# A hybrid DeltaNet and sliding-window decoder layer: the framework sorts each engine's instructions by its finer clock instead of its simple one

## The chip, the cores and the metric

The kernel runs on one core of a Trainium2 chip. The core has engines that each work through their own list of instructions in order: PE (matrix products), ACT (scalar functions), DVE (vector operations), POOL (a second, slower vector engine) and SP, which issues all DMA transfers of this kernel. An instruction that waits holds up everything behind it on its engine. The metric is the time of one execution in microseconds (us) on the device; the time of a kernel is the median of its runs.

## The reference, cut to what matters

The layer takes x (2048 rows of 1024) and computes, in fp32:

```
xn  = rms_norm(x)                                # 2048 x 1024
p   = xn @ w_in                                  # q,k,v of the DeltaNet, z gates, q,k,v of attention, branch gates
A   = gated delta rule over chunks of 64 (conv, l2 norm, triangular solve, scan over the chunks), 4 heads
B   = dilated sliding-window attention, 4 heads x 3 groups (dilation 1, 4, 16), merged by their softmax denominators
y   = sigmoid(g0) * ((norm(A) * silu(zA)) @ w_branch_dn) + sigmoid(g1) * ((B * silu(zB)) @ w_branch_swa)
out = x + y @ w_out
```

## The kernel before, in words

The program text is a list of stages. Every large product is done in three passes on two-part operands (a high part `hh`, `wh`, `oh`, `mh` and a rest `hl`, `wl`, `ol`, `ml`), which stand as three lines each in the profile.

1. **Attention** (`swa`): 12 units (3 groups x 4 heads) of 16 steps. A step projects 128 rows to q, k and v with 24 products of 128x384 (`s_proj`, L176 to L178, into a tile `mm`), normalises them (`s_norm`), and takes earlier rows through the attention in small pieces between the products: transposes of q and k (`a_trans`, L231, tile `tp`), scores (`a_score`, L249 to L251, or L246 in the last group, tile `sc`), row maximum on DVE (L253, L256), the exponential on ACT (L258, tile `p`), transposes of `p` (`a_ptrans`, L265), a copy of them on ACT (L267, tile `pT`), the product with v (`a_pv`, L273 and L274, tile `po`), a copy and a store (L276, L279). The weights of the next unit come meanwhile as 256 KB pieces (tile `raw`, three buffers) and are split into two parts by ACT (L79) and by DVE or POOL (L80).
2. **Column units** (`cunits`): 36 units of 128 columns of `w_in`, four blocks of 512 rows each, 24 products of 128x512 a block (L413 to L415). Small work is hung between these products by a table of events: the last attention items, the DeltaNet's gates (`ab_math`), for each of four heads the convolution (L510 to L521), the transposes of k (L552, tile `tp`, taken on by ACT in L556 and L557) and the k and q products (L598 to L601), the triangular inverse on DVE, the scan (16 steps: L729 and L731, L740, L746, L751 on PE, L733, L748 and L754 on DVE, L736, L742 and L758 on ACT, a store in L769).
3. **Prologue of the end**: when the scan has stored its last rows, its memory is given to the end stage. `o_load` loads a tile of DeltaNet output (`od`, L861) and one of attention output (`oc`, L838, one buffer), `combine` merges the three groups on DVE (L843 to L855, tile `osw`), `o_prep` transposes both (L870), multiplies them by the gates z (L871) and splits them (L874 on ACT, L875 on POOL) into `oh` and `ol`. Beside it the weights of the end are loaded in 32 pieces (L824, `raw` and `raw2`, three buffers each) and split (L831 on ACT, L833 on DVE or POOL) into the memory of `hh` and `hl`, which the column units read until their last blocks.
4. **End**: eight blocks of 256 rows; `fin_y` has 24 products of 128x256 for each of eight column blocks (L886 to L888, then L890 on DVE, L893, L894), `fin_out` the output product (L903 to L905) and the store (L910).

Dependencies become semaphores, and tiles with a few buffers make a later instruction wait for the last reader of the buffer. The framework does not keep the order of the text: it simulates the engines with a clock and hands out, of the instructions that are ready on its clock, the one of the highest priority; the order in which they come out is the fixed order of each engine's list. PSUM tiles are few: `mm` has 3 buffers, `tp` 2, `sc` 2, `po` 1.

```python
            a["kqT"] = self.sp.tile([P, 2, P], F32, name="kqT", bufs=1)
...
        oc = fp.tile([P, G, H, 130], F32, name="oc", bufs=1)
...
        raw = self.fp.tile([P, 4, P], F32, name="raw2", bufs=3) if k0 else self.rawp.tile([P, 4, P], F32, name="raw")
```

## Time and profile before

| | |
|---|---|
| time, median of 3 runs | 2415.41 us (2414.24 to 2415.93) |
| the profiled execution | 2419.78 us, 4.37 us above the median |
| its span, first to last instruction | 2417.9 us |
| granted clock of PE, mean | 0.993 |
| instructions on PE | 13710 products and as many weight loads |
| busy | PE 98%, DVE 48%, ACT 35%, POOL 34% of the span |

In the profiled execution the attention runs from the start to about 1003 us, the column units from there to about 2030 us (their products are mixed with the last attention items until about 1140 us, the four heads until about 1460 us, the inverse until about 1740 us, the scan until about 1916 us, the prologue of the end until about 1952 us) and the end stage from 2030 us on. Rows of the profile are read thus: a start time, a duration, the engine, the line and the operation, what is written and what is read, and in square brackets the idle time of the engine just before with what ended it. Since products overlap on PE, the time from one start to the next is what a product costs, not its duration.

### The profile page before, as it was taken

What the parts mean: (1) busy time and instruction counts of PE and PEld (TensorE: products, weight loads), DVE (VectorE), ACT (ScalarE), POOL (GpSimd) and SP (SyncE); (2) the same over time, 40 slices, a digit from 0 to 9 for tenths busy, and PEclk for the clock granted to TensorE, in tenths of its full rate; (3) what the DMA queues carried; (4) which work ended last, traced back from release to release, by engine and by line L of the source; (5) the groups of instructions that cost most, each with busy time, mean ns of one, the idle gap of its engine ahead of it and who ended that gap; (6) DMA issues with size and microseconds to landing.
All of it is one profiled execution on the core that took longest, in us unless ns stands there. A gap on an engine that the chain in (4) does not pass through costs nothing.

```text
span 2417.9 us, 40142 instructions
## 1 busy us (share of the span) xinstructions
PE 2365.4 (98%) x13710; PEld 2151.0 (89%) x13710; DVE 1163.6 (48%) x2738; ACT 848.3 (35%) x2985; POOL 824.2 (34%) x1785
## 2 busy tenths in 40 slices
PE   7999999999999999999999999999999999999999
PEld 7999999999999999987777878888888878889998
DVE  5644433233343433343766665999444433454431
ACT  5644433243443333322665662111243313111110
POOL 4433334433333343420433541111133212442441
PEclk9999999999999999999999999999999999999999
DMA  5211102233333333433444443222566655555542
GB/s 158 76 44 39 31 23 66 92 98 95 113 104 96 109 114 96 108 104 97 128 121 123 112 115 111 79 75 72 179 199 195 184 162 155 160 182 156 151 139 75
DMA packets 348819, 274.22 MB, mean 113 GB/s; under 512 B 57864, under 2 KB 317256, under 8 KB 348232
## 3 DMA queue, kind: packets, MB, share of 16 engines
q1 hardware_dynamic: 348616, 271.66, 38.7%
q8 instruction: 109, 1.79, 0.3%
q14 instruction: 94, 0.77, 0.1%
HBM read 167.47 MB, written 104.10 MB: 112 GB/s over the span
## 4 chain that ended last, share of the span: by engine, by line
PE 83%; DMA 6%; DVE 4%; ACT 3%; POOL 2%; issue 2%; SPq 1%; DVEq 0%; ACTq 0%; POOLq 0%
PE mm L176 10%; PE mm L178 10%; PE mm L177 10%; PE mm L413 9%; PE mm L415 8%; PE mm L414 8%; PE mm L903 2%; PE mm L905 2%; PE mm L904 2%; PE mm L886 2%; PE mm L888 2%; DMA gcb<-gcscr 2%; PE mm L887 2%; PE po L274 2%; PE tp L231 2%
## 5 line engine op out<-in xcount | busy, mean ns | idle before, releaser
L176 PE MATMUL mm<-wh,hh 128*128 128x384 f32 (+1 forms) x1536 | 555.5, 362 | 2.7 <-ACT hh L119 2.0
L178 PE MATMUL mm<-wh,hl 128*128 128x384 f32 (+1 forms) x1536 | 521.0, 339 | 0.0
L177 PE MATMUL mm<-wl,hh 128*128 128x384 f32 (+1 forms) x1536 | 520.6, 339 | 0.2 <-POOL wl L80 0.2
L413 PE MATMUL mm<-hh,wh 128*128 128x512 f32 x1152 | 468.0, 406 | 0.0
L415 PE MATMUL mm<-hh,wl 128*128 128x512 f32 x1152 | 457.1, 397 | 0.0
L414 PE MATMUL mm<-hl,wh 128*128 128x512 f32 x1152 | 454.6, 395 | 0.0
L176 PEld LDWEIGHTS mm<-wh,hh 128*128 128x128 f32 x1536 | 291.4, 190 | 5.7 <-ACT hh L119 2.4
L177 PEld LDWEIGHTS mm<-wl,hh 128*128 128x128 f32 x1536 | 292.2, 190 | 0.6 <-POOL wl L80 0.6
L178 PEld LDWEIGHTS mm<-wh,hl 128*128 128x128 f32 x1536 | 290.7, 189 | 0.0
L415 PEld LDWEIGHTS mm<-hh,wl 128*128 128x128 f32 x1152 | 218.6, 190 | 47.1
L413 PEld LDWEIGHTS mm<-hh,wh 128*128 128x128 f32 x1152 | 219.0, 190 | 44.3
L414 PEld LDWEIGHTS mm<-hl,wh 128*128 128x128 f32 x1152 | 218.9, 190 | 42.0
L80 POOL TENSOR_TENSOR wl<-raw,wh 128x512 fp32r<-128x512 f32 (+1 forms) x75 | 107.5, 1445 | 406.0 <-ACT wh L79 405.8
L199 DVE SCALAR_TENSOR_TENSOR rec<-mm,st,wqk 128x128 f32<-128x128 f32 x256 | 78.0, 347 | 265.0 <-POOL st L197 256.0
L195 POOL TENSOR_SCALAR st<-st 128x2 f32<-128x2 f32 x192 | 45.2, 235 | 424.3 <-ACT rec L191 288.8
L258 ACT ACTIVATE p<-sc,ol 128x128 f32<-128x128 f32 (+1 forms) x192 | 81.9, 427 | 297.8 <-DVE ol L256 284.1
L886 PE MATMUL mm<-oh,hh 128*128 128x256 f32 x512 | 143.9, 281 | 3.0 <-DVE gt L890 3.0
L888 PE MATMUL mm<-oh,hl 128*128 128x256 f32 x512 | 143.0, 279 | 0.0
L887 PE MATMUL mm<-ol,hh 128*128 128x256 f32 x512 | 143.0, 279 | 0.0
L518 DVE SCALAR_TENSOR_TENSOR acc<-xr,cw,acc 128x512 f32<-128x512 f32 x144 | 121.7, 845 | 42.3 <-ACT acc L516 38.2
L197 POOL TENSOR_TENSOR st<-st,mhalf 128x2 f32<-128x2 f32 x192 | 134.7, 701 | 16.0
L79 ACT ACTIVATE wh<-raw 128x512 fp32r<-128x512 f32 (+1 forms) x145 | 90.0, 631 | 110.2 <-PE mm L414 73.8
(240 smaller groups left out, 4317.9 us busy)
## 6 DMA issues: line engine op xcount, KB each, us to landing
raw<-in_w_in_dram SPq DMA_DIRECT2D x144, 256.0 KB, 3.4
rscr<-rec SPq DMA_DIRECT2D x128, 192.0 KB, 1.9
qk<-rscr SPq DMA_DIRECT2D x128, 128.0 KB, 2.2
gscr<-gt SPq DMA_DIRECT2D x64, 256.0 KB, 2.4
gt<-gscr SPq DMA_DIRECT2D x64, 256.0 KB, 3.5
oscr<-ol SPq DMA_DIRECT2D x192, 65.0 KB, 1.9
oc<-oscr SPq DMA_DIRECT2D x16, 780.0 KB, 5.6
rec<-rec SPq DMA_DIRECT2D x16, 768.0 KB, 5.4
```

The lines of the kernel that those rows point to most:

```text
L80: eng.tensor_tensor(out=l, in0=raw, in1=h.bitcast(F32), op=ALU.subtract)
L176: nc.tensor.matmul(pr[:, :w], a, wh[:, k, :w], start=(k == 0), stop=False)
L177: nc.tensor.matmul(pr[:, :w], a, wl[:, k, :w], start=False, stop=False)
L178: nc.tensor.matmul(pr[:, :w], b, wh[:, k, :w], start=False, stop=(k == KT - 1))
L197: nc.gpsimd.tensor_tensor(out=st[:, 2:4], in0=st[:, 0:2], in1=self.mhalf[:, 0:2], op=ALU.pow)
L413: nc.tensor.matmul(pr, wh[:, k, :], a, start=(k == 0), stop=False)
L414: nc.tensor.matmul(pr, wh[:, k, :], b, start=False, stop=False)
L415: nc.tensor.matmul(pr, wl[:, k, :], a, start=False, stop=(k == KT - 1))
L518: nc.vector.scalar_tensor_tensor(out=acc, in0=xr[:, j:j + 512], scalar=w[:, j:j + 1], in1=acc, op0=ALU.mult, op1=ALU.add)
L886: nc.tensor.matmul(o, self.wbh[:, k, ms], oh[:, k, :], start=(k == b * 4), stop=False)
L887: nc.tensor.matmul(o, self.wbh[:, k, ms], ol[:, k, :], start=False, stop=False)
L888: nc.tensor.matmul(o, self.wbl[:, k, ms], oh[:, k, :], start=False, stop=(k == b * 4 + 3))
```

## The change

One argument is added, which makes the framework's sorting use another clock: one that models instructions and transfers with finer durations, the transfers' among them.

```diff
     out = nc.dram_tensor("out_0_dram", (1, T, D), F32, kind="ExternalOutput").ap()
-    with tile.TileContext(nc) as tc:
+    with tile.TileContext(nc, schedule_with_timeline_sim=True) as tc:
         with ExitStack() as ctx:
             Net(ctx, tc, ins, out).run()
```

The instructions stay the same: 12897 products and transposes on PE, 1354 transfers, and the same operations on DVE, ACT and POOL. What changes is their order on each engine, and with it which of them carry a wait. Three places of the new order follow. A name with a number is one buffer's use (`po_6588`), `x2` stands for two like instructions in a row.

**Place 1, attention, in the seventh unit, on PE.** `mm_6551` and `mm_6620` are the projections of two successive steps; L273 and L274 multiply `pT_6561` (made by ACT in L267) with v. Before:

```order
L176 MATMUL mm_6551<-wh_5841,hh_67 128x384
L177 MATMUL mm_6551<-wl_5842,hh_67 128x384
L178 MATMUL mm_6551<-wh_5841,hl_68 128x384
L273 MATMUL po_6588<-v_6220,pT_6561 128x128
L274 MATMUL po_6588<-v_6290,pT_6561 128x128
L231 MATMUL tp_6593<-ident_69,qk_6427 128x128 x2
```

The same product in the new order:

```order
L178 MATMUL mm_6620<-wh_5841,hl_68 128x384
L176 MATMUL mm_6620<-wh_5841,hh_67 128x384
L177 MATMUL mm_6620<-wl_5842,hh_67 128x384
L273 MATMUL po_6588<-v_6220,pT_6561 128x128
L274 MATMUL po_6588<-v_6290,pT_6561 128x128
L265 MATMUL tp_6627<-ident_69,p_6580 128x128 x2
```

It has moved from one step's projection into the next step's, behind 20 more products of 128x384 in all; between the transposes `tp_6558` (L265), from which `pT_6561` is copied, and L273 stand 21 projection products and two transposes now, where there were 12 and three score products.

On ACT, the copy L267 and the splits L79 of the next unit's weights at that place, before:

```order
L79 ACTIVATE wh_6963<-raw_7180 128x4x128
L191 ACTIVATE rec_6536,st_6535<-mm_6484 128x128 x2
L192 ACTIVATE rec_6536<-mm_6484 128x128
L79 ACTIVATE wh_6963<-raw_7253 128x4x128
L267 ACTIVATE pT_6561<-tp_6558 128x256
L79 ACTIVATE wh_6963<-raw_7326 128x4x128
```

and now:

```order
L79 ACTIVATE wh_6963<-raw_7180 128x4x128
L258 ACTIVATE p_6512,ol_6509<-sc_6505,ol_6509 128x256
L191 ACTIVATE rec_6536,st_6535<-mm_6484 128x128 x2
L192 ACTIVATE rec_6536<-mm_6484 128x128
L79 ACTIVATE wh_6963<-raw_7253 128x4x128
L79 ACTIVATE wh_6963<-raw_7326 128x4x128
L267 ACTIVATE pT_6561<-tp_6558 128x256
```

One more split and one exponential stand ahead of the copy.

**Place 2, the last attention items, on PE, among the column units.** Before, with blocks of column products between the pieces:

```order
L274 MATMUL po_13788<-v_13575,pT_13763 128x128
L231 MATMUL tp_13792<-ident_69,qk_13665 128x128 x2
L413 MATMUL mm_13754<-hh_67,wh1_13493 128x512
L414 MATMUL mm_13754<-hl_68,wh1_13493 128x512
L415 MATMUL mm_13754<-hh_67,wl1_13494 128x512
L413 MATMUL mm_13754<-hh_67,wh1_13493 128x512
L414 MATMUL mm_13754<-hl_68,wh1_13493 128x512
L415 MATMUL mm_13754<-hh_67,wl1_13494 128x512
L265 MATMUL tp_13805<-ident_69,p_13780 128x128
```

Now:

```order
L415 MATMUL mm_14116<-hh_67,wl1_13749 128x512
L274 MATMUL po_13735<-v_13526,pT_13710 128x128
L246 MATMUL sc_13775<-kqT_13742 128x128
L265 MATMUL tp_13761<-ident_69,p_13727 128x128
L231 MATMUL tp_13792<-ident_69,qk_13665 128x128 x2
L274 MATMUL po_13788<-v_13575,pT_13763 128x128
L246 MATMUL sc_13824<-kqT_13795 128x128
L265 MATMUL tp_13805<-ident_69,p_13780 128x128
L231 MATMUL tp_13841<-ident_69,qk_13712 128x128 x2
L274 MATMUL po_13837<-v_13617,pT_13807 128x128
```

The items have moved behind later column blocks (`mm_14116`, where they stood in `mm_13754`), and the last nine follow one another with no column product between them.

**Place 3, the end of the scan, on PE and DVE.** L746 is the scan's last product, L870 the transposes for the end, L886 the end's first product. Before, on PE, the last product of the scan:

```order
L746 MATMUL po_20970<-vn_20957,rec_20800 128x128 x2
L751 MATMUL tp_20954<-vn_20957,rec_20800 128x128 x2
L751 MATMUL tp_20959<-vn_20962,rec_20800 128x128 x2
L746 MATMUL po_20990<-vn_20962,rec_20800 128x128 x2
L413 MATMUL mm_20947<-hh_67,wh1_20030 128x512
```

then 492 column products, with the first four tiles' L870 behind 78, 84, 96 and 108 of them, and at last:

```order
L414 MATMUL mm_21708<-hl_68,wh1_21504 128x512
L415 MATMUL mm_21708<-hh_67,wl1_21505 128x512
L886 MATMUL mm_21784<-oh_21151,hh_67 128x256
L887 MATMUL mm_21784<-ol2_21152,hh_67 128x256
L888 MATMUL mm_21784<-oh_21151,hl_68 128x256
```

Now, in one piece:

```order
L415 MATMUL mm_21708<-hh_67,wl1_21505 128x512
L740 MATMUL tp_20959<-rr_20933,vb1_18949 128x128 x2
L746 MATMUL po_20970<-vn_20957,rec_20800 128x128 x2
L751 MATMUL tp_20954<-vn_20957,rec_20800 128x128 x2
L751 MATMUL tp_20959<-vn_20962,rec_20800 128x128 x2
L746 MATMUL po_20990<-vn_20962,rec_20800 128x128 x2
L870 MATMUL tp_21155<-ident_69,od_21023 128x128 x4
L870 MATMUL tp_21173<-ident_69,osw_21035 128x128 x4
L870 MATMUL tp_21199<-ident_69,od_21103 128x128 x4
L886 MATMUL mm_21784<-oh_21151,hh_67 128x256
```

`mm_21708` is the last column block. The scan starts where it started and ends right behind the last column product; the first product of the end follows it directly. 36 products of the end come next, and only then the L870 of `osw_21115`, the second attention tile. On DVE the updates of the state (L748) and of the output (L754) in the last step, before:

```order
L733 SCALAR_TENSOR_TENSOR rr_20933<-sc_20931,ksn_13082,rec_20800 128x128 x2
L748 SCALAR_TENSOR_TENSOR S0_18940<-S0_18940,eglb_13080,po_20970 128x128
L748 SCALAR_TENSOR_TENSOR S1_18941<-S1_18941,eglb_13080,po_20970 128x128
L754 TENSOR_TENSOR qs_20921<-tp_20954,qs_20921 128x256
L754 TENSOR_TENSOR qs_20932<-tp_20959,qs_20932 128x256
```

and now:

```order
L733 SCALAR_TENSOR_TENSOR rr_20933<-sc_20931,ksn_13082,rec_20800 128x128 x2
L833 TENSOR_TENSOR hl_68<-raw_21893,hh_67 128x4x128
L833 TENSOR_TENSOR hl_68<-raw_21901,hh_67 128x4x128
L833 TENSOR_TENSOR hl_68<-raw_21940,hh_67 128x4x128
L833 TENSOR_TENSOR hl_68<-raw_21979,hh_67 128x4x128
L748 SCALAR_TENSOR_TENSOR S0_18940<-S0_18940,eglb_13080,po_20970 128x128
L748 SCALAR_TENSOR_TENSOR S1_18941<-S1_18941,eglb_13080,po_20970 128x128
L754 TENSOR_TENSOR qs_20921<-tp_20954,qs_20921 128x256
L833 TENSOR_TENSOR hl_68<-raw_22036,hh_67 128x4x128
L754 TENSOR_TENSOR qs_20932<-tp_20959,qs_20932 128x256
```

Splits of the output weights (L833, pieces `raw_...` in three buffers, each split by ACT in L831 first) stand ahead of the scan's last updates; before they stood behind the end's first L890. The splits of the `raw2` pieces stand likewise among the rows of `combine`. In the four heads, in the stretch between places 2 and 3, the second to fourth pairs of L552 of heads two to four stand 1.1 to 4 us of products later on PE than before, and L600 1.8 to 2.5 us later; the column units under the inverse keep their order.

## The prediction

> **What bounds the kernel.** I read the page's first lines and its chain, then the waits of PE, then tables by stage.
>
> ```profile
> span 2417.9 us, 40142 instructions
> PE 2365.4 (98%) x13710; PEld 2151.0 (89%) x13710; DVE 1163.6 (48%) x2738; ACT 848.3 (35%) x2985; POOL 824.2 (34%) x1785
> PE 83%; DMA 6%; DVE 4%; ACT 3%; POOL 2%; issue 2%; SPq 1%; DVEq 0%; ACTq 0%; POOLq 0%
> ```
>
> PE is busy 2365 of 2418 us and makes up 83% of the chain that ends last; every other engine is idle over half of the span. The new order gives PE the same products. So only two things can change the time: the idle 52.5 us, with what the clock loses behind them, and idle time that the new order makes. The waits of PE (engine, line, what it waited for; us in total, times, longest):
>
> ```profile
> PE tp L552 <- ACT st L557: 8.8, 5, 2.9
> PE po L273 <- ACT pT L267: 7.1, 5, 2.0
> PE mm L116 <- DVE qk L199: 3.9, 5, 1.7
> PE tp L870 <- DVE osw L855: 3.5, 1, 3.5
> PE tp L265 <- ACT p L258: 2.8, 4, 2.0
> PE po L274 <- ACT pT L267: 2.3, 2, 1.2
> PE sc L600 <- POOL kql L588: 1.7, 1, 1.7
> PE tp L740 <- DVE rr L733: 1.0, 1, 1.0
> ```
>
> They are short and spread over all stages. The next table has stretches with window, length, PE busy (the other engines follow), and the granted clock ahead of the last two columns:
>
> ```profile
> 20.00:130.00 110.00, 105.55 (x687) 101.51 (x685) 71.53 (x162) 64.83 (x210) 54.67 (x129) 1.00 0.33 95
> 380.00:1000.00 620.00, 610.39 (x3775) 603.91 (x3774) 226.97 (x804) 226.65 (x1010) 248.31 (x714) 0.99 0.35 102
> 1160.00:1460.00 300.00, 287.69 (x1400) 236.15 (x1399) 199.04 (x323) 188.14 (x596) 133.70 (x206) 0.98 0.46 119
> 1930.00:1960.00 30.00, 26.50 (x112) 21.46 (x112) 16.18 (x36) 6.15 (x13) 7.71 (x6) 0.89 0.92 272
> 2040.00:2080.00 40.00, 34.98 (x223) 30.05 (x222) 16.29 (x22) 13.38 (x25) 20.77 (x22) 0.96 0.63 176
> ```
>
> Idle in these five are 4.5, 9.6, 12.3, 3.5 and 5.0 us; what the clock fell short, length times missing share, adds about 6, 6, 3.3 and 1.6 us to the last four. That is where there is something to win: some 52 us in all.
>
> **Why a stall costs more than its length.** One attention stall, PE and ACT:
>
> ```profile
> 541.53 0.34 PE L177 MATMUL mm<-wl,hh 128*128 128x384 f32 x1
> 541.70 0.34 PE L178 MATMUL mm<-wh,hl 128*128 128x384 f32 x1
> ...
> 542.24 0.34 PE L178 MATMUL mm<-wh,hl 128*128 128x384 f32 x1
> 544.45 0.49 PE L273 MATMUL po<-v,pT 128*128 128x128 f32 x2 [1.88 <-ACT pT L267]
> ...
> 545.71 0.53 PE L178 MATMUL mm<-wh,hl 128*128 128x384 f32 x1
> ...
> 548.59 0.44 PE L178 MATMUL mm<-wh,hl 128*128 128x384 f32 x1
> ...
> 542.30 0.63 ACT L79 ACTIVATE wh<-raw 128x512 fp32r<-128x512 f32 x1 [2.93 <-DMA raw<-in_w_in_dram]
> 543.49 0.64 ACT L79 ACTIVATE wh<-raw 128x512 fp32r<-128x512 f32 x1
> 544.01 0.39 ACT L267 ACTIVATE pT<-tp 128x256 f32<-128x256 f32 x1
> ```
>
> Starts lie 0.17 us apart before, and after two idle us nine of them take 2.88 us instead of 1.57: another 1.3 us. The reader sees also whose fault it is: ACT sat behind a weight split (L79) whose transfer was late, and the copy L267 that PE needs stood behind it.
>
> **The change part by part.** Each term is the change of the profiled execution's time.
>
> *Start, 20 to 130 us.* The transposes L116 wait for DVE's L199, 3.9 us. The new order sets them further behind their producers. **-4** (0 to -4.5).
>
> *Attention, 380 to 1000 us.* L273 moves 20 products, 3.5 us, later at the place shown, more than the stall there (2.2 us less the product's own 0.17); the split (0.63 us above) and the exponential (0.37 for half its size, below) that now pass ahead of L267 on ACT eat a third of that. L273 and L274 wait thus seven times. The transfer behind L79 is not faster, so a later start of it would bring the stall back. I let 7.5 of 9.6 us go and 4.5 of the 6 that the clock lost: **-12** (0 if the loads slip as far as the copies, -15 at most).
>
> *Last attention items and first head, 1003 to 1160 us.* The nine items that now stand without column products between them are a chain: the transposes L265 of an item need the exponential of the scores L246 just ahead.
>
> ```profile
> 1056.61 0.39 PE L246 MATMUL sc<-kqT 128*128 128x128 f32 x2
> ...
> 1057.03 0.30 DVE L253 CUSTOM_DVE_ANT_0 sc<-sc,mask 128x128 f32<-128x128 f32 x1 [0.18 <-PE sc L246]
> ...
> 1057.63 0.37 ACT L258 ACTIVATE p<-sc,ol 128x128 f32<-128x128 f32 x1 [0.54 <-DMA qk<-rscr]
> ```
>
> From L246 to the end of L258 are 1.4 us; PE's own work for one item, five small products, is about 0.6 us (a larger one takes 0.118, below). Nine items at 1.45 instead of 0.62 us cost 7.5 us. The stalls of today's end go in exchange (L265, 2.0 of its 2.8 us, and its slow stretch, 1.3 as above), and the first head's transposes, which start later against DVE's convolution, may wait: I put 1 us for them, bounds 0 and 8. **+5** (+2 to +12).
>
> *Heads two to four, 1160 to 1460 us.* Three of L552's stalls reach 2.4 to 2.9 us, and the 6 us of the clock are theirs, 2 each. That line moves 1.1 to 4 us later, which leaves less than 2 us each (the gap of 2.0 us above is the shortest behind which I found a slow stretch): 3 x (1.1 + 2) = 9.3; L600, moved too, has 1.7 more, and ACT's own order can take some back. **-9** (-3 to -12).
>
> *Scan.* L740's 1.0 us goes with the wider spacing. **-1.**
>
> *The end of the scan.* Here an advantage of the old order is lost. The chain behind the last product of the scan, as it runs now:
>
> ```profile
> 1915.56 0.68 PE L746 MATMUL po<-vn,rec 128*128 128x128 f32 x4
> ...
> 1929.72 0.17 DVE L843 TENSOR_REDUCE cs<-oc 128x4 f32<-128x12 f32 x1 [4.21 <-DMA oc<-oscr]
> ...
> 1933.76 0.69 DVE L855 TENSOR_TENSOR osw<-osw,oc 128x512 f32<-128x512 f32 x1
> 1933.93 0.60 PE L870 MATMUL tp<-ident,od 128*128 128x128 f32 x4
> ...
> 1939.35 0.17 DVE L843 TENSOR_REDUCE cs<-oc 128x4 f32<-128x12 f32 x1 [4.03 <-DMA oc<-oscr]
> ...
> 1945.00 0.69 DVE L855 TENSOR_TENSOR osw<-osw,oc 128x512 f32<-128x512 f32 x1
> ...
> 1948.44 0.62 ACT L874 ACTIVATE oh<-z 128x512 fp32r<-128x512 f32 x1
> ...
> 1948.33 2.55 POOL L80 TENSOR_TENSOR wl<-raw,wh 128x512 fp32r<-128x512 f32 x2
> 1950.83 1.29 POOL L875 TENSOR_TENSOR ol<-z,oh 128x512 fp32r<-128x512 f32 x1
> ```
>
> The scan's last product ends at 1916.2. Its rows go to DRAM and the memory changes hands; `oc` is there at 1929.7; the first attention tile is merged at 1934.45, and only then is its one buffer free for the second, merged at 1945.7; the second half of the first end products can start at 1952.1. That is 35.9 us, of which POOL's unrelated L80 accounts for 1.7: **34.2 us**. Today 108 column products stand on PE ahead of the last of these transposes and 384 behind it, so it costs one stall of 3.5 us. In the new order no column product is left behind the scan: PE has 16 transposes (four in 0.6 us with the last one's tail, so some 2 us) and 36 products of the end. Their pitch:
>
> ```profile
> 2045.75 0.28 PE L886 MATMUL mm<-oh,hh 128*128 128x256 f32 x1
> ...
> 2047.99 0.28 PE L887 MATMUL mm<-ol,hh 128*128 128x256 f32 x1
> ```
>
> 19 starts in 2.24 us, 0.118 each, so 36 take 4.3 us and all 6.3. Loss 34.2 - 6.3 = **28**, hard to escape.
>
> To it come the splits L833 that now stand on DVE ahead of the scan's last L748, and on ACT (L831) ahead of its last `vn`. Eight pieces go through three buffers, and their memory is free only when the column blocks that read it are done.
>
> ```profile
> raw<-in_w_out_dram SPq DMA_DIRECT2D x16, 256.0 KB, 4.8
> ```
>
> A round of three is a transfer of 4.8 us, a split on ACT (0.63, as L79 above) and one on DVE (0.7, as L855): 6.1 us. The last two pieces ahead come in a third round: about 5 us later than the scan alone. The `raw2` splits among the rows of `combine` can do the same twice: between 0 and 12 us, I take 5. Two restarts after long idle times at a slow clock: 3 us, as in the stretch 1930 to 1960. Loss 28 + 5 + 5 + 3 = 41. In exchange goes what this and the next stage lose today, 3.5 + 3.3 + 5.0 + 1.6 = 13.4, since the end's weights are split during the long wait. **+27.5** (+15 to +40).
>
> **Sum.** -4 - 12 + 5 - 9 - 1 + 27.5 = **+6.5**. The profiled execution took 2419.78 us (span 2417.9), so 2426.3; it lay 4.4 us above the median of the runs shown, 2415.41, and I take that off: **2422**. About 0.2%, 4.8 us, is what a measurement of this kernel can tell from no change.
>
> **Rivals.**
>
> *A: the gains win.* If the split pieces have landed early, the end of the scan costs its floor (28 + 2 - 13 = +17 with two short restarts), and attention and heads give their best: -4 - 15 + 2 - 12 - 1 + 17 = -13, **2402**. For it: every moved attention row has its distance grown, and DMA is 0.35 and 0.46 busy in the two stages. Against it: three buffers and the columns' memory force rounds.
>
> *B: slower, the splits decide.* The place is DVE's list at the scan's end. If each of three places there (ahead of L748, within the first `combine`, within the second) waits for a whole round of 6.1 us, that is 18.3 instead of my 10, and the fourth group of end products, whose `mm` buffer is freed by an L890 that now stands behind the third `combine`, waits a round more: +14.4, **2436**. It decides from the point where a `raw2` piece lands later than `oc` does.
>
> *C: the attention stalls move along with the weight loads*, since ACT's splits still stand ahead of L267 and the raw buffers come free no sooner: 0 for -12, **2434**. For it: the transfer, not the order, was late at 542.30.
>
> *D: the slow stretches are not the gaps' doing and stay*, so that a gap of 2 us gives back its length alone: 4.5 and 6 us less are won, **2432**. The rows behind 544.45 speak against it. [...]
>
> *E: nothing is seen*, the order differs but all of it is hidden: **2415**. The 28 us at the end of the scan speak against it, since PE's list has nothing to hide them with.
>
> **How the numbers follow.** Forecast 2422 with its own range 2413 to 2430: 0.43 (0.26 slower, 0.17 within 0.2%). A 0.25 (0.22 faster, 0.03 within). B 0.17, C 0.08 and D 0.02, all slower. E 0.05, within. Faster 0.22, within 0.25, slower 0.53. The range leaves out the lower 40% of A and of B and C the upper 40%: 2400 to 2438.
>
> **What would show it.** Right: an idle PE of some 20 us before the first L886 and a second one of some 10 us before the L870 of the second `osw`, with the clock low behind both; waits of L273 on L267 below 3 us in all, and of L552 below 4; 6 to 9 us of short waits of L265 on L258 around 1130 to 1145 us. Wrong: if the gaps before L886 come to less than 20 us together (A), if L833 on DVE waits over 12 us between the scan's last L733 and the second L855 (B), or if L273's waits stay at 7 us (C). The forecast fails altogether if a stage that I left at nothing, the columns under the inverse or the end after its first block, has new waits.

## The result, and the profile after

| | before | after |
|---|---|---|
| time, median | 2414.82 us (2412.98 to 2415.93, 4 runs) | 2428.87 us (2426.53 to 2433.24, 4 runs) |
| the profiled execution | 2419.78 us | 2433.24 us |
| granted clock of PE, mean | 0.993 | 0.988 |

The ratio is **1.0058, 95% interval 1.0046 to 1.007**: the new order makes the kernel 0.6% slower. The prediction was 2422 us, range 2400 to 2438, with slower the likeliest. The profile of after is the slowest of its four runs, that of before 4.4 us above the median of the runs shown with it.

The first lines of the page of after, and its chain:

```profile
span 2431.1 us, 40236 instructions
PE 2363.2 (97%) x13710; PEld 2145.9 (88%) x13710; DVE 1162.0 (48%) x2738; ACT 838.6 (34%) x2985; POOL 828.3 (34%) x1785
PE 78%; DMA 10%; DVE 6%; ACT 2%; issue 2%; POOL 2%; SPq 0%; DVEq 0%; ACTq 0%; POOLq 0%
```

PE has the same work, but its part of the chain fell from 83% to 78%, and DMA's and DVE's rose by 4 and 2 points. The waits of PE (engine, line, what it waited for; us in total, times, longest):

```profile
PE tp L870 <- DVE osw L855: 11.0, 2, 10.3
PE tp L870 <- DMA od<-odn: 9.2, 1, 9.2
...
PE tp L552 <- ACT st L557: 6.6, 6, 2.3
PE sc L600 <- POOL ss L569: 5.3, 1, 5.3
...
PE mm L886 <- DVE ot L909: 3.6, 4, 1.9
PE mm L887 <- POOL ol L875: 2.8, 2, 1.7
PE mm L886 <- DVE gt L890: 2.2, 3, 1.3
PE tp L265 <- ACT p L258: 1.8, 3, 0.6
...
PE po L274 <- ACT pT L267: 0.4, 1, 0.4
...
PE po L273 <- ACT pT L267: 0.3, 1, 0.3
```

The waits for L267 are gone (9.4 us before); waits at the end of the scan, one in the first head (L600) and a new kind in the end stage (L886 for L909) have come. The stages in the same table as before (window, length, PE busy, the other engines, clock, DMA share, GB/s), with the end of the scan where it now lies:

```profile
20.00:130.00 110.00, 109.40 (x724) 107.52 (x723) 71.47 (x168) 65.61 (x220) 55.33 (x133) 1.00 0.34 98
380.00:1000.00 620.00, 619.11 (x3870) 611.49 (x3869) 230.33 (x825) 225.22 (x1032) 251.08 (x734) 1.00 0.36 104
1160.00:1460.00 300.00, 286.68 (x1395) 235.11 (x1394) 201.53 (x325) 187.75 (x606) 132.94 (x200) 0.97 0.48 119
1960.00:2040.00 80.00, 57.49 (x341) 48.80 (x340) 35.77 (x87) 29.55 (x86) 16.12 (x41) 0.86 0.60 187
2040.00:2080.00 40.00, 32.00 (x214) 30.16 (x215) 28.98 (x48) 10.93 (x23) 24.33 (x23) 0.86 0.62 187
```

The start and the attention lose almost nothing any more (0.6 and 0.9 us idle, clock 1.00), and 1960 to 2080 has 30.5 idle us at a clock of 0.86. For a balance by stage I give PE's list a **lag**: the time at which a product starts in the trace, less the sum of the pitches at full clock of all that stands ahead of it on PE (distances of starts in the trace of before: 0.1745 us for 128x384, 0.229 for 128x512, 0.118 for 128x256, 0.1095 for a transpose and 0.222 for another product with 128 columns, which leaves two records). Both kernels have the same products and the same pitches, so the difference of the lags is what a stage gained or lost. The last column has the kernels below that keep the new order in the stage:

| stage (edges in us of PE's list) | forecast | after less before | other profiles |
|---|---|---|---|
| start (to 88) | -4 | -5.6 | -3.9 to -5.5 |
| attention (88 to 1003) | -12 | -15.3 | -15.7 to -17.5 |
| last items (1003 to 1103) | +4 | +3.5 | +2.8 to +3.4 |
| first head (1103 to 1242) | +1 | +9.2 | +6.9 to +8.2 |
| heads two to four (1242 to 1670) | -9 | -4.1 | -3.6 to -7.2 |
| scan, and the old stall at L870 (1670 to 1939) | -1 and -6.8 | -8.8 | -9.2 |
| loss at the end of the scan (1939 to 1952) | +41 | +35.9 | +35.1 to +36.3 |
| the old stalls behind it (1952 to 1985) | -6.6 | -6.6 | -7.2 to -8.1 |
| the end after its first block (1985 on) | 0 | +4.9 | +5.9 to +7.0 |
| sum | +6.5 | +13.1 | |

Two cautions. A stage's lag differs from profile to profile: in `old_to_inverse` (below) the attention stands in the old order, and its lag is still 3.5 us below that of the profile of before. And the edge at 1103 falls at 1136 us of the trace of after, inside a stretch in which the granted clock is 0.50 (1133.4 to 1140.2 us, from the last items on), so some 1.7 us of the first head's +9.2 belong to the items.

The end of the scan, PE and DVE of after in the timeline (start, duration, engine, line; idle time before, and its releaser):

```profile
2015.23 0.65 PE L746 MATMUL po<-vn,rec 128*128 128x128 f32 x4
2025.11 1.08 PE L870 MATMUL tp<-ident,od 128*128 128x128 f32 x4 [9.23 <-DMA od<-odn]
2036.50 1.09 PE L870 MATMUL tp<-ident,osw 128*128 128x128 f32 x4 [10.31 <-DVE osw L855]
...
2040.60 1.01 PE L886 MATMUL mm<-oh,hh 128*128 128x256 f32 x3 [2.15 <-ACT oh L874]
2043.30 0.58 PE L887 MATMUL mm<-ol,hh 128*128 128x256 f32 x1 [1.69 <-POOL ol L875]
...
2050.27 0.63 PE L870 MATMUL tp<-ident,osw 128*128 128x128 f32 x4 [0.67 <-DVE osw L855]
...
2055.41 0.58 PE L887 MATMUL mm<-ol,hh 128*128 128x256 f32 x1 [1.08 <-POOL ol L875]
...
2027.32 0.17 DVE L843 TENSOR_REDUCE cs<-oc 128x4 f32<-128x12 f32 x1 [4.14 <-DMA oc<-oscr]
...
2029.90 2.97 DVE L852 TENSOR_TENSOR oc<-oc,cs 128x512 f32<-128x512 f32 x3
2032.79 1.75 DVE L833 TENSOR_TENSOR hl<-raw,hh 128x512 fp32r<-128x512 f32 x1
...
2035.67 0.68 DVE L855 TENSOR_TENSOR osw<-osw,oc 128x512 f32<-128x512 f32 x1
...
2042.07 0.17 DVE L843 TENSOR_REDUCE cs<-oc 128x4 f32<-128x12 f32 x1 [1.19 <-DMA oc<-oscr]
...
2049.43 0.69 DVE L855 TENSOR_TENSOR osw<-osw,oc 128x512 f32<-128x512 f32 x1
```

It is the chain of before with nothing to cover it. From the end of the scan's last product (2015.88) to the product that needs the second half (2055.41) are 39.5 us, against 35.9 before. Link by link, after against before: to the landed `oc` 11.4 against 13.5, its merge 9.0 against 4.7, to the second `oc` 5.7 against 4.9, its merge 8.1 against 6.3, to L887 5.3 against 6.4. The two merges are 6.0 us longer, with splits of weights (L833) between their rows.

One statement ahead of the prediction was loose: the attention's projections do not end at about 1003 us but, mixed with the first column blocks, at 1047 us in the profile of before and 1027 in that of after.

### The profile page after: what moved, and what is told of

Its sections match the earlier page's. It is cut to its first block, busy times and chain, and to the rows that moved or that the text cites. A ratio compares the mean times of both kernels' runs of the same rounds, so it can differ in the third digit from the quotient of the medians.

```text
span 2431.1 us, 40236 instructions
## 1 busy us (share of the span) xinstructions
PE 2363.2 (97%) x13710; PEld 2145.9 (88%) x13710; DVE 1162.0 (48%) x2738; ACT 838.6 (34%) x2985; POOL 828.3 (34%) x1785
## 4 chain that ended last, share of the span: by engine, by line
PE 78%; DMA 10%; DVE 6%; ACT 2%; issue 2%; POOL 2%; SPq 0%; DVEq 0%; ACTq 0%; POOLq 0%
PE mm L177 11%; PE mm L176 11%; PE mm L178 11%; PE mm L415 8%; PE mm L413 8%; PE mm L414 8%; DMA gcb<-gcscr 3%; PE po L274 2%; DMA z<-zscr 2%; PE tp L231 2%; DMA oc<-oscr 2%; PE mm L886 1%; PE mm L888 1%; PE mm L887 1%; PE tp L265 1%
## 5 line engine op out<-in xcount | busy, mean ns | idle before, releaser
L176 PE MATMUL mm<-wh,hh 128*128 128x384 f32 (+1 forms) x1536 | 543.3, 354 | 1.6 <-ACT hh L119 1.6
L178 PE MATMUL mm<-wh,hl 128*128 128x384 f32 (+1 forms) x1536 | 534.0, 348 | 0.0
L413 PE MATMUL mm<-hh,wh 128*128 128x512 f32 x1152 | 461.6, 401 | 0.3 <-ACT acc L516 0.3
L176 PEld LDWEIGHTS mm<-wh,hh 128*128 128x128 f32 x1536 | 290.0, 189 | 3.7 <-ACT hh L119 2.0
L195 POOL TENSOR_SCALAR st<-st 128x2 f32<-128x2 f32 x192 | 39.0, 203 | 406.3 <-ACT rec L191 268.0
L267 ACT ACTIVATE pT<-tp 128x128 f32<-128x128 f32 (+1 forms) x192 | 64.9, 338 | 270.3 <-PE tp L265 270.2
L886 PE MATMUL mm<-oh,hh 128*128 128x256 f32 x512 | 145.0, 285 | 10.3 <-ACT oh L874 4.5
L887 PE MATMUL mm<-ol,hh 128*128 128x256 f32 x512 | 144.8, 283 | 2.8 <-POOL ol L875 2.8
L276 DVE COPY ol<-po 128x128 f32<-128x128 f32 x192 | 55.4, 288 | 181.5 <-PE po L274 181.5
```

Of the source, the lines that this page charges most:

```text
L176: nc.tensor.matmul(pr[:, :w], a, wh[:, k, :w], start=(k == 0), stop=False)
L178: nc.tensor.matmul(pr[:, :w], b, wh[:, k, :w], start=False, stop=(k == KT - 1))
L413: nc.tensor.matmul(pr, wh[:, k, :], a, start=(k == 0), stop=False)
L886: nc.tensor.matmul(o, self.wbh[:, k, ms], oh[:, k, :], start=(k == b * 4), stop=False)
L887: nc.tensor.matmul(o, self.wbh[:, k, ms], ol[:, k, :], start=False, stop=False)
```

## The experiments

All kernels below have the flag, and so the same instructions and buffers; what differs is the order. It is fixed by an edge of issue order from each instruction to the one before it on its engine, along a table:

```diff
-            Net(ctx, tc, ins, out).run()
+            net = Net(ctx, tc, ins, out); net.run(); pin(nc, tc)
+def pin(nc, tc):
+    made = {i.name: i for i in nc.cur_bb.bb.instructions}
...
+        for a, b in zip(seq, seq[1:]):
+            tc.add_manual_dep(made[b], a, mybir.DependencyInfo(mybir.DependencyClass.NoSync,
+                                                               mybir.DependencyReason.DATA), reason="pin")
```

So an order can be composed by stages: instructions that start before a cut time in the trace of before stand as in one order, those behind it as in the other.

**1 to 3. Which stages win, which lose.** `new_attention`: the new order up to 1003 us, the old behind. `new_to_inverse`: new up to 1480 us, old behind. `old_to_inverse`: old up to 1480 us, new behind.

> Every engine's list is pinned: what starts before 1003 us in the profile of the kernel before (the attention units) stands in the new order, all the rest in the old one. Theory (the two orders differ stage by stage, and each stage keeps its gain or loss): the attention and the start give 20.9 us, as the two profiles' PE stand at that point, so 2394 us against 2415, ratio 0.991. Rival (PE only runs ahead there and waits for the same late engines and transfers afterwards): the gain is given back in the heads, 2402 to 2415 us.

> New order up to 1480 us of the profile of before (attention, its last items, the four heads), old order behind it (inverse, scan, end). Theory: 12.3 us faster, 2402.5, that is 8.6 us slower than with the new order in the attention alone, since the last items and the first head lose 12.3 and heads two to four win 4.0. Rival (the loss behind 1003 us is not of this stretch's order): as fast as with the attention alone, 2394.

> Old order up to 1480 us of the profile of before, new order behind it. Theory: the end of the scan and the end stage lose 25.5 us net by themselves, 2440 us, ratio 1.0106. Rival (the new order's PE meets its waits there only because it arrives 12 us earlier than the transfers and DVE allow): about as fast as the whole new order or faster, 2428 or less.

Measured: 2395.48 us (ratio 0.9917, 0.9903 to 0.9931), 2399.46 (0.9934, 0.992 to 0.9947) and 2440.9 (1.0105, 1.0091 to 1.0118). The attention alone gains 0.8%, the items and heads behind it give a little back, and everything from the inverse on costs 1.05%. Together they give +0.4%, just within their intervals of the 0.6% measured. That is the change in two numbers, and the prediction's main statement: the gain lies ahead of the inverse, the loss behind.

**4. `mix_heads`.** Four cuts: new order in the attention (to 1040 us), old in the last items and the first head (to 1228), new in heads two to four (to 1480), old behind.

> Pinned by the profile of before: new order up to 1040 us (attention), old up to 1228 (last items, first head), new up to 1480 (heads two to four), old behind. Theory (each stretch keeps its own gain): 4 us less than with the new attention alone, about 2391.5. Rival (heads two to four win only because their new order follows a first head that ends later): 2395.5 or more.

Measured: **2384.84 us, ratio 0.9879 (0.9865 to 0.9892)**: 30 us below before, 44 below after and 7 below what was expected, the best of the case. Its busy times and its chain:

```profile
PE 2348.0 (99%) x13710; PEld 2137.3 (90%) x13710; DVE 1163.5 (49%) x2738; ACT 836.4 (35%) x2985; POOL 821.1 (34%) x1785
...
PE 89%; DMA 5%; DVE 2%; ACT 2%; issue 1%; POOL 1%; SPq 0%; DVEq 0%; ACTq 0%; POOLq 0%
```

PE's part of the chain is 89%. Its busy time is 17 us less than in before, for the same products: they run less often at a low clock (0.999 granted in the mean, 0.993 in before).

**5. Who holds up L600 in the first head?** The waits name POOL (L569). The timeline of after, PE and DVE:

```profile
1182.09 0.55 PE L600 MATMUL sc<-kql,kqh 128*128 128x256 f32 x1 [5.27 <-POOL ss L569]
...
1178.16 1.61 DVE L539 TENSOR_TENSOR gcb<-gcb,cmask 128x512 f32<-128x512 f32 x1 [2.49 <-ACT acc L516]
...
1181.26 0.68 DVE L590 TENSOR_TENSOR kql<-qT,kqh 128x512 fp32r<-128x512 f32 x1
```

L600 reads `kql`, and L590, which writes it, ends at 1181.94, 0.15 us ahead of L600. L590 stands behind L539, which waits 2.49 us for a tile that it has nothing to do with. The edit of DVE's list (`kql_14383`):

```diff
+L590 TENSOR_TENSOR kql_14383<-qT_14368,kqh_14382 128x4x128
 L539 TENSOR_TENSOR gcb_14856<-gcb_14856,cmask_13073 128x512
 L543 SCALAR_TENSOR_TENSOR gcb_14856<-gcb_14856,ngc_13076 128x128 x2
-L590 TENSOR_TENSOR kql_14383<-qT_14368,kqh_14382 128x4x128
```

> The new order with one instruction moved: in the first head, on DVE, L590 (the rest of q, second block, kql_14383) stands ahead of L539, which waits for a transfer of gcb, instead of four rows behind it. In the profile of the new order PE stood 5.27 us before L600, and the waits name POOL's L569, while L590 ended 0.15 us before L600 started. Theory (DVE's place decides): the gap falls to about 1 us (POOL's L588 ends 1177.9) and the slow clock behind it goes, 6 us less than the new order, ratio to before about 1.0033. Rival (POOL, as the waits say: L569 behind two L80): no change, 1.0058.

Measured: 2422.7 us, ratio 1.0027 (1.0015 to 1.0039), 6 us below after by the medians, and the wait of 5.3 us for L569 is not among PE's waits any more (1.6 us for L588 have come). The stage's lag is 15.3 us, against 17.6 to 19.9 in the five other profiles with this order, so 2 to 5 of the 6 us are shown to be this row's. DVE's list was the cause; POOL's row was only the last event that the view found.

**6. The end after its first block.** The new waits of L886 for L909 (3.6 us, four times) have the same shape: on DVE the copy that frees PE's `mm` buffer stands behind the rows of the next tile's merge, which wait for their transfer.

```profile
2150.97 0.18 DVE L843 TENSOR_REDUCE cs<-oc 128x4 f32<-128x12 f32 x1 [5.86 <-DMA oc<-oscr]
...
2154.34 0.68 DVE L909 SCALAR_TENSOR_TENSOR ot<-mm,xo 128x512 f32<-128x512 f32 x1
```

`new_ot_first` moves it ahead of them, in four places:

```diff
+L909 SCALAR_TENSOR_TENSOR ot<-mm,xo 128x512
 L843 TENSOR_REDUCE cs<-oc 128x4
...
 L852 TENSOR_TENSOR oc<-oc,cs 128x4x128 x3
-L909 SCALAR_TENSOR_TENSOR ot<-mm,xo 128x512
```

> The new order with four instructions moved: in the end stage, on DVE, the last L909 of four blocks (the output tile ot, whose read frees an mm buffer) stands ahead of the second combine's nine rows, which wait for a transfer of oc, instead of behind them. Theory: PE's waits of L886 on L909 (3.6 us in four) go, with the clock behind the longest: 4 us less than the new order, ratio about 1.0041. Rival (the combine then ends later and its transposes wait instead): no change, 1.0058.

Measured: 2422.67 us, ratio 1.0033 (1.0021 to 1.0046). The lag behind 1985 us is 1.8 instead of 4.9, so 3 us are shown to be L909's place; the other 3 us of the ratio come from stages that this edit doesn't touch. So two unlike edits of a few rows both measure 6 us below after. No run has the new order pinned and otherwise unchanged, so what pinning does by itself is not known; that is why only the edited stage's lag is counted for an edit.

**7. The splits among the merges.** `new_splits_behind` sets the four `raw2` splits on DVE behind the merges they stand in, and moves the second `oc` load and the operands of the fourth transposes (on ACT and POOL) ahead likewise:

```diff
 L852 TENSOR_TENSOR oc_21025<-oc_21025,cs_21027 128x4x128 x3
+L854 TENSOR_TENSOR osw_21035<-oc_21025 128x512
+L855 TENSOR_TENSOR osw_21035<-osw_21035,oc_21025 128x512
 L833 TENSOR_TENSOR hl_68<-raw2_21663,hh_67 128x4x128
-L854 TENSOR_TENSOR osw_21035<-oc_21025 128x512
 L833 TENSOR_TENSOR hl_68<-raw2_21687,hh_67 128x4x128
-L855 TENSOR_TENSOR osw_21035<-osw_21035,oc_21025 128x512
```

> The new order with the splits of raw2 pieces at the end of the scan moved behind the two combines: L833 on DVE behind each L855, L845, L871, L874 and L875 of the second tile ahead of the splits on DVE, ACT and POOL, and the second load of oc ahead of three loads of raw2. Theory (the splits among the rows of combine cost what I took, 5 us and the slow rows of combine beside POOL's splits): 6 us less than the new order, ratio about 1.0033. Rival (the chain is transfers and combine alone, the splits stand in its gaps): 0 to 1 us. Against both: the weights come later to the first end products, which could then cost up to 6 us more.

Measured: 2435.44 us, ratio 1.0087 (1.0073 to 1.01), slower than after. The loss at the end of the scan falls from 35.9 to 32.4, but the next stretch (1952 to 1960) loses 12.5 instead of 1.6, with this row among PE's waits:

```profile
PE mm L886 <- DVE gt L890: 11.7, 2, 10.6
```

and this on DVE:

```profile
2052.82 0.69 DVE L833 TENSOR_TENSOR hl<-raw,hh 128x512 fp32r<-128x512 f32 x1 [3.86 <-ACT hh L831]
...
2062.49 0.67 DVE L890 SCALAR_TENSOR_TENSOR gt<-gt,mm 128x512 f32<-128x512 f32 x1
```

The splits, with the load and the operands that moved along, cost 3.5 us where they stand. Moved, they hold up something else: L886 waits for a buffer of `mm`, and L890, which frees it, stands on DVE behind splits that wait for their halves from ACT (3.86 us, then 1.09) and behind the third merge. In after the same L890 starts at 2061.50, and PE waits 1.35 us for it. In the two orders tried, DVE's list serves one of these demands at the cost of the other.

**8. Is the half clock behind an idle time due to the idleness, and does it cost anything here?** `new_warm` fills PE's idle times at the end of the scan with transposes nobody reads:

```diff
+            warm = net.ps.tile([P, 512], F32, name="sc", bufs=2)
+            for n in range(172):
+                nc.tensor.transpose(warm[:, :P], net.ident, net.ident)
```

> The new order, and PE multiplies the identity with itself (172 extra transposes of 128x128 into a spare PSUM tile, whose result nobody reads) in the idle times at the end of the scan: 66 before the first L870, 70 before the second, 14 and 8 around the first L886, 14 before the second group of L886. Theory (the half clock behind an idle time is due to the idleness): the 21 starts behind the first L887, 0.213 us apart in the new order, come 0.118 us apart (-2.0 us), the 13 in the second stretch too (-1.2), and the L870 ahead of them takes half (-0.4): some 3.6 us less than the new order, ratio to before 1.0043 instead of 1.0058; PE's lag at the end of the scan 32 to 33 us instead of 36. Rival (the slow pace belongs to the place, for example to the transfers beside it): starts stay 0.21 us apart, no gain, or up to 3 us lost where the extra transposes stand in the way.

Measured: 2429.86 us, ratio 1.0067 (1.0055 to 1.0079): no gain. PE in its timeline (the added transposes read `ident` alone):

```profile
2030.86 1.09 PE L870 MATMUL tp<-ident,osw 128*128 128x128 f32 x4 [3.01 <-DVE osw L855]
...
2032.60 2.36 PE L1059 MATMUL sc<-ident 128*128 128x128 f32 x14
2034.96 0.62 PE L886 MATMUL mm<-oh,hh 128*128 128x256 f32 x3
...
2037.69 0.39 PE L887 MATMUL mm<-ol,hh 128*128 128x256 f32 x1 [1.24 <-POOL ol L875]
...
2041.56 0.28 PE L888 MATMUL mm<-oh,hl 128*128 128x256 f32 x1
2044.66 1.09 PE L870 MATMUL tp<-ident,osw 128*128 128x128 f32 x4 [2.82 <-DVE osw L855]
```

The clock did as the theory said: the products behind L887 start 0.12 us apart, 3.9 us from L887 to the last of them, against 6.0 in after (2043.30 to 2049.32). But the gain turned into a wait: L870 of the second attention tile now waits 2.82 us for DVE instead of 0.67, and from one `osw` transpose to the next it is 13.8 us in both kernels. The second merge sets the time there, not PE's clock.

**9. What mends the attention: the split ahead of the copy, or the distance on PE?** `old_copy_first` keeps the old order and changes only ACT's list, in 22 places such as:

```diff
-L79 ACTIVATE wh_1392<-raw_1400 128x4x128
 L191 ACTIVATE qk_1374,st_1373<-mm_1309 128x128 x2
 L192 ACTIVATE v_1375<-mm_1309 128x128
 L267 ACTIVATE pT_1418<-tp_1415 128x256
+L79 ACTIVATE wh_1392<-raw_1400 128x4x128
```

> The old order, but on ACT, in 22 places of the attention where one to three splits L79 stand directly (or with only L191 and L192 between) ahead of a copy L267, the copy goes ahead of them. Theory (the splits, whose transfers are late, hold the copy up, and that is what the new order mends in the attention): the seven waits of L273 and L274 for L267, 9.4 us, go, and 3 to 5 us of slow clock behind them: 2403 us, ratio 0.995 (0.9940 to 0.9965). Rival 1 (it is the distance on PE from the transposes L265 to L273 that the new order mends, the copy is late by itself): 0 to -3 us, ratio 0.9988 to 1.0. Rival 2 (the splits, now later, hand the wait on to the projections that need wh): waits of L176 or L177 for L79 or L80 appear, ratio 0.998 to 1.002.

Measured: 2409.11 us, ratio 0.998 (0.9971 to 0.9988): 6.3 us by the medians, of the 12 that the theory promised. Rival 1 gave 3 at most; rival 2's sign is not there, since L176 waits 0.8 us for L79 as it did in before. The waits for L267 are gone from PE's list, but the exponential L258 now stands behind the late splits:

```profile
PE tp L265 <- ACT p L258: 5.4, 8, 1.3
```

(2.8 us, four times, before). The attention's lag falls by 10.5 us, where the new order takes 15.3; but by 3.5 it falls in `old_to_inverse` too, without any edit there. So the late split on ACT is a cause of the old stalls, as the prediction read it, worth about 6 us, and taking one victim out of its way leaves the next. That the larger distances on PE bring the rest is what remains as an explanation; no run has them alone.

**10 and 11. Could the scan be spread only as far as needed?** From the inverse on, `blend_80` and `blend_60` sort `mix_heads`'s lists by a mean of the start times in the two traces, with a weight of 0.8 and 0.6 for before:

```
tail.sort(key=lambda n: lam * start_before[n] + (1 - lam) * start_after[n])
```

> mix_heads, but from the inverse on each engine's list is sorted by 0.8 times the start time in the old order plus 0.2 times that in the new: the scan's steps stand wider apart than in the old order, and some 384 column products are left behind the scan instead of 504. Theory (the old order's scan is packed too tightly for its own chain and loads, which costs PE 18 us between the inverse and the scan's end, against 10 with the new order's spacing; the reserve of columns behind the scan needs only the 34 us of the chain): 3 to 5 us less than mix_heads, 2380 to 2382 us, ratio 0.9858. Rival (the lists blended in this way bring waits that neither order had): 2385 to 2395 us.

> As blend_80 with 0.6 and 0.4: some 282 column products are left behind the scan, 64 us, still more than the chain of 34 us. Theory: 5 to 8 us less than mix_heads, 2377 to 2380 us, ratio 0.985, with no wait of L886 above 3 us at the scan's end. Rival 1 (blended lists bring new waits): 2385 to 2395 us. Rival 2 (the chain with its loads and splits does not fit into the 64 us): waits of L870 or L886 of more than 5 us and 2385 us or more.

Measured: 2399.67 us (0.9935, 0.9922 to 0.9948) and 2411.08 us (0.9984, 0.9974 to 0.9995). Both are slower than `mix_heads`, and the theory falls. What held is the reserve: 376 and 256 column products stand behind the scan's last product, and the loss from 1939 to 1952 us of PE's list is 2.0 and 3.8 us, where after, with none, has 35.9. New waits are one part of what was lost, with a sign that both rivals of `blend_60` name. The longest of them, in `blend_60`:

```profile
PE mm L886 <- DVE gt L890: 8.4, 1, 8.4
```

(7.0 in `blend_80`; in both, L890 stands on DVE behind splits L833 that wait for ACT.) The larger part lies in the scan, which did not get cheaper: between 1670 and 1900 us of PE's list it loses 30.5 and 26.9, against 17.9 in `mix_heads`, at a granted clock of 1.00 and with 4.2, 0.3 and 4.2 us idle in the trace from 1670 to 1970 us. Up to 1830 us of the list PE changes 401, 387 and 99 times between column products and the scan's, which are 397, 351 and 448 there; the lag is 25.3, 20.4 and 14.3. So it goes with the number of changes, not with the pace of the steps, as I had thought.

The starts on PE show which changes cost. L707 and L715 are 64x64 products that prepare a step of the scan. In `mix_heads` their records stand together in groups of eight, 32 groups up to 1830 us of the list; the blended lists tear them into 65 and 58 groups, as here in `blend_80`:

```profile
1730.07 0.49 PE L414 MATMUL mm<-hl,wh 128*128 128x512 f32 x1
1730.49 0.33 PE L715 MATMUL sc<-vb,zs 64*64 64x64 f32 x2
1730.74 0.49 PE L746 MATMUL po<-vn,rec 128*128 128x128 f32 x2
```

From the column product's start to that of L715 are 0.42 us, where the pitch is 0.229, and from there to L746 0.25, where the pitch of two records of L715 is 0.117. With the record ahead of a group and the one behind it, a group costs 0.34 to 0.35 us above the pitches, in before, after, `mix_heads` and both blends alike. For 32, 65 and 58 groups these are 10.9, 23.0 and 20.3 us of the lag, and all the rest is below 4 us in each. So the torn groups account for the blends' loss in the scan; no run has a blended list with the groups left whole.

## Why the prediction was right, and where not

**The direction was right, for the reason given.** The new order wins in the attention and the heads and loses at the end of the scan, where nothing is left on PE behind the scan's last rows. Runs 1 to 3 show both sides apart, run 4 shows that they can be had apart. The size was not right: +6.5 us were forecast for the profiled execution and +13.1 came. The last items and the heads cost 12.6 us more than forecast and the end after its first block 4.9, and the start, the attention, the scan and its end 11 less. That these errors cancel in part is luck.

**Start and attention** (-4 and -12): -5.6 and -15.3; mis-sized by 5 us together, in the change's favour. C, the stalls moving along with the loads, is out: L273's waits fell to 0.3 us. Run 9 shows that C named a real cause, the late split; that the larger distance on PE does the rest is argued, not shown.

**Last items** (+4 of the +5): +3.5. The nine items cost what the chain of 1.45 us said, but not as the waits of L265 that I listed (1.8 us seen, 6 to 9 named):

```profile
1131.05 0.49 PE L274 MATMUL po<-v,pT 128*128 128x128 f32 x2
...
1132.49 0.49 PE L274 MATMUL po<-v,pT 128*128 128x128 f32 x2
...
1134.47 0.79 PE L274 MATMUL po<-v,pT 128*128 128x128 f32 x2 [0.37 <-ACT pT L267]
```

Items follow 1.3 to 2.0 us apart, and most of that time counts as PE's own (busy 7.96 of the 9.70 us from 1122.79 to 1132.49), where the view of waits shows none.

**First head** (+1, bounds 0 and 8): +9.2 in the profile of after, or 7.5 without the slow clock that the items leave behind, so at the upper bound. The step that failed: I looked for the cost at the transposes L552, whose producers are DVE's convolution, and not at L600, whose operand L590 stands in DVE's list behind another head's waiting row. Run 5 shows 2 to 5 us of it.

**Heads two to four** (-9): -4.1 in the profile of after, -3.6 to -7.2 in the others; the right mechanism, sized too large. L552 still waits 6.6 us where I wanted less than 4. The 2 us below which I counted nothing for the clock are no threshold: in after it fell behind gaps that had lasted 0.37 us at most (last section).

**The end of the scan** (+41 of loss, -13.4 given back): +35.9; given back 6.6 behind it and about 6.4 ahead, near the 6.6 and 6.8 forecast. The floor of 28 held. Of what I put on top: 5 for a third round of splits ahead of the scan's last products was too much (PE waits 1.3 us there, for `vn`); 5 for the splits in the merges was near (the merges are 6.0 us longer, and 3.5 come off the loss in run 7); 3 for the slow restarts was wrong. Run 8 shows that they hide behind the second merge (13.8 us from one `osw` transpose to the next, with and without them). I charged PE's clock at a place where PE is not the bound.

**The end after its first block** (0): +4.9. This was named as something at which the forecast fails, and it did fail there: DVE's list in that stage is new as well, and I had not looked at it. In the sum the 5 us by which the end of the scan was overrated hide it, which is luck; the time would lie in the wide range without that too.

**The rivals.** A needed the floor to be the whole loss: it was 28 of 36. B needed waits of whole rounds: there were none, though its place was the right one. D: behind 1.88 us of idle time in before and 3.01 in `new_warm` the granted clock is 0.50 for 3.41 us, and behind L887, where `new_warm` fills idle time ahead, the starts are 0.12 us apart instead of 0.21; in run 9 the stretch at the old stall is gone with the stall (starts 0.17 us apart behind a wait of 1.25 there).

**What stays open.** Why the finer clock spreads the scan over all the columns. In the new order 45 to 50 column products stand between two steps of the scan, 18 in the old. That was not tried on the chip. Of the 32.4 us left when the splits are out of the merges, 28 are the floor; no run takes the other 4 apart.

## What to carry to other kernels

An order that is better by a finer clock can lose all its gain at one place: see what each stage leaves on the bounding engine for the latency of the stage behind it, and keep that reserve (here 34 us of column products). Judge an order by stages, each against its own trace, and compose the parts: the best kernel here takes two stages from the new order and the rest from the old. And behind a wait, look at what stands ahead of the producer on its engine before you believe the releaser's name.

## What the runs showed of the hardware that was not expected

**The half clock lasted 3.41 us or a whole multiple of it.** In `new_warm` the four transposes that start at 2030.86, behind 3.01 idle us, take 1.09 us, where four take 0.63 at 2019.58, behind 1.59. The granted clock there (window, length, PE busy, the other engines, clock, DMA share, GB/s):

```profile
2027.14:2030.55 3.41, 0.71 (x7) 0.47 (x5) 3.41 (x5) 0.40 (x1) 1.22 (x1) 1.00 0.86 266
2030.55:2033.96 3.41, 3.10 (x15) 3.13 (x16) 1.61 (x3) 1.25 (x3) 0.54 (x1) 0.50 1.06 321
2033.96:2037.37 3.41, 2.49 (x20) 2.01 (x18) 1.03 (x3) 1.47 (x3) 3.41 (x3) 1.00 0.87 292
```

The return falls among the fourteen added transposes at 2032.60: the first seven start 0.213 us apart, the last seven 0.109. In before the half clock lasts from 545.39 to 548.80, behind 1.88 idle us; in after it lasts nine such lengths in one piece, from 2017.40 to 2048.12, over idle times of 9.23, 10.31, 2.15 and 1.69 us. Of the fifteen half-clock stretches in these two profiles (without the one in each that the end of the execution cuts off) eleven last 3.41 us, two 6.83, one 10.24 and one 30.72. One gap's length does not tell whether it falls: behind 1.24 idle us (L887 at 2037.69) it stays full, behind 1.73 in before (L600 at 1188.79) too, and in after it falls at 1133.35, where no gap in the 3.41 us ahead had lasted longer than 0.37. PE was busy 0.71 us of the 3.41 ahead of the fall in the table and 1.53 ahead of that at 545.39, 0.61 to 2.38 ahead of the fifteen in before and after; 3.10 ahead of the return in the table, 2.92 to 3.41 ahead of those in before and after. But it was busy 2.49 where the clock stayed full in `new_warm`, and only 1.72 where it did so in before (1187.10 to 1190.51). Where the limit lies no run shows.

**DVE's L852 and L833 took longer beside POOL's rows.** L852 takes 2.97 us for three in the first merge and 1.90 in that of before, and L833 1.75 against 0.69 at 2011.32, where no such row of POOL ran beside it, while POOL ran these:

```profile
2030.53 1.79 POOL L875 TENSOR_TENSOR ol<-z,oh 128x512 fp32r<-128x512 f32 x1 [11.16 <-ACT oh L874]
2032.35 1.64 POOL L833 TENSOR_TENSOR hl<-raw,hh 128x512 fp32r<-128x512 f32 x1
```

In the second merges it is the other way round: 1.90 us for the three L852 in after (at 2045.19), with a row of POOL beside only their last 0.3 us (2046.79), and 2.97 in before (at 1941.39), beside an L875 of POOL (1941.82).

**A group of 64x64 products cost PE 0.34 to 0.35 us that no wait shows** (runs 10 and 11), whether it has eight records or two: 12.1 us for the 33 groups more of `blend_80`. Changes between 128x512 and 128x128 products cost nothing that the lag shows: the blends have over 220 more of them than `mix_heads`, and their rest (the lag less the groups' share) is 2.3 and 0.1 us, against 3.4.
